# Two padding tiles in a one-core trunk kernel: where the tiles that TensorE reads begin in a partition

## Chip, core and metric

The program runs on one core of one Trainium2 chip. The metric is device time in microseconds (us) of one execution, from the launch to the end; lower is better. A profiled execution has a span too: the time from the first to the last instruction that the hardware profiler recorded. Engines are named as in the profile: PE is TensorE's matmul side, PEld its weight loads, DVE is VectorE, ACT is ScalarE, POOL is GpSimd, SP is SyncE, which here issues nearly all DMAs.

## What is computed

A decoder trunk of two layers on a sequence of 256 tokens with 1024 features, all in 32-bit floats. Each layer is half a SwiGLU feed-forward block, a mixer, and another half feed-forward block; layer 0 mixes by latent attention beside a pooling mixer, layer 1 by a causal spatial gate:

```python
def _swiglu(x, w_gate, w_up, w_down):
    return (jax.nn.silu(x @ w_gate) * (x @ w_up)) @ w_down

for layer in range(DEPTH):                       # DEPTH = 2
    h = h + 0.5 * _swiglu(_rmsnorm(h, ffn_norm[layer, 0]), ...)   # 1024 -> 2816 -> 1024
    hn = _rmsnorm(h, mix_norm[layer])
    h = h + (_mla_pool_mixer(hn, ...) if layer % 2 == 0 else _spatial_gating_mixer(hn, ...))
    h = h + 0.5 * _swiglu(_rmsnorm(h, ffn_norm[layer, 1]), ...)
```

## The kernel before

Everything is held transposed: features lie on the 128 partitions and the 256 tokens along them. The kernel keeps 32-bit accuracy by splitting each operand in two values of type float32r, a rounded high part and a low part that is the rest. A weight chunk arrives from HBM in a tile `raw` of 128 x 1024 floats (`emit_dma`, L148, issued by SP), ACT casts it to `whi` (`emit_hi`, L160, L169), and DVE subtracts to get `wlo` (`emit_split`, L171, L177). There are five buffers of `raw` and six each of `whi` and `wlo`; `next_chunk` (L196) keeps this pipeline some chunks ahead of the use. The activations are split likewise: a tile `x` holds for each of eight feature blocks the low part and then the high part, 256 tokens each. `pp` is the same for the hidden layer of a feed-forward block, `comb` and `zz` for the mixers (they use the buffers of `x`).

Two helpers make nearly all products. `mm2` (L214) serves the feed-forward blocks. It issues two matmuls for each weight block of 128 columns: one with `wlo` as the stationary operand and the 256 columns of the high activations moving (L216), and one with `whi` stationary and all 512 columns, low and high, moving (L217). `mm3` (L209) serves the mixers, with three matmuls of equal width (L210, L211, L212). In most of them weights are stationary and 256 activation columns move; in the three input products with the names `lat`, `kv`/`q` and `v` the activations are stationary and 416, 512, 384 or 512 weight columns move. Each matmul has a weight load of its own. A feed-forward block runs 352 pairs of `mm2` for gate and up (`gate_up`, L341) and 176 for down (`down`, L388); there are four such blocks, so 2112 pairs in all.

The order of instructions is the order of the code (a manual schedule). Tiles come out of pools, and a pool hands out bytes of a partition in the order in which the tiles are first asked for: `const`, then `weights` (`raw`, `whi`, `wlo`), then `acts` (`x`), then `small`, and behind them the pools that live for one block (`pp`, `gu` and `a` in a feed-forward block, the mixers' tiles otherwise). A tile that is added to `const` shifts all that stands behind it.

Of the kernel before, what the change touches and what calls it, by code (L numbers as in the profile page):

```python
# [9 lines left out]
F32 = mybir.dt.float32  # L10
# [6 lines left out]
P = 128  # L17
# [59 lines left out]
def trunk_kernel(  # L77
# [24 lines left out]
    const = ctx.enter_context(tc.tile_pool(name="const", bufs=1))  # L102
    wpool = ctx.enter_context(tc.tile_pool(name="weights", bufs=1))
    xpool = ctx.enter_context(tc.tile_pool(name="acts", bufs=1))
    spool = ctx.enter_context(tc.tile_pool(name="small", bufs=2))
# [916 lines left out]
        return nxt  # L1022


    wu = const.tile([P, T], mybir.dt.bfloat16, name="wu")
    nc.vector.memset(wu, 0.0)
    warm_ps = acc_bank()
# [118 lines left out]
```

## Time and profile before

| | us |
|---|---|
| device time, median of 3 runs (lowest, highest) | 909.73 (909.56, 912.51) |
| device time of the profiled execution | 912.56 |
| its span | 910.8 |
| outside the span | 1.8 |
| PE busy | 899.7 |
| DVE busy | 645.5 |
| ACT busy | 496.4 |

Matmuls overlap in the pipeline, so "busy" counts an engine with at least one matmul in flight. How fast PE goes is read from the starts: the distance between the start of one matmul and the start of the next is what one costs in a stream. The timeline has these starts to 0.01 us, so a distance is best taken over many rows. The recorded duration of a single matmul (281 ns or 399 ns, say) is longer than this distance, since it holds the way through the pipeline.

### The profile page before, as it was taken

How to read it: one execution, taken by the hardware profiler on the slowest of the kernel's cores; microseconds unless marked ns; L12 is line 12 of the kernel's file. 1: busy time of each engine (PE TensorE's matmuls, PEld its weight loads, DVE VectorE, ACT ScalarE, POOL GpSimd, SP SyncE). 2: the span in 40 equal slices, each digit the busy share in tenths (PEclk: the TensorE clock that was granted, in tenths of full speed). 3: DMA queues.
4: the chain of work that ended last, by engine and by line, in shares of the span. 5: the costliest groups of instructions: out<-in, count | busy, mean ns of one | idle time of the engine just before them, and what ended most of it. 6: DMA issues, size and time to landing. Idle time of an engine off the chain costs nothing.

```text
span 910.8 us, 13887 instructions
## 1 busy us (share of the span) xinstructions
PE 899.7 (99%) x5320; PEld 790.6 (87%) x5320; DVE 645.5 (71%) x973; ACT 496.4 (55%) x782; POOL 99.5 (11%) x130
## 2 busy tenths in 40 slices
PE   8999999999999999999999999999999999999998
PEld 6888888899898888888888888888899988888887
DVE  7787778668877877785558777756658768777652
ACT  8555554447675555554446555544445655555430
POOL 4200000017524000000030000000120220000000
PEclk9999999999999999999999999999999999999999
DMA  8575555634344655556544555576446446555740
GB/s 290 189 241 192 195 178 192 210 120 159 116 140 139 203 182 190 178 188 234 192 157 141 185 185 185 185 258 185 157 148 202 144 160 206 188 186 186 248 162 23
DMA packets 59281, 164.45 MB, mean 181 GB/s; under 512 B 5456, under 2 KB 7760, under 8 KB 59216
## 3 DMA queue, kind: packets, MB, share of 16 engines
q1 hardware_dynamic: 59216, 163.58, 53.3%
q8 instruction: 41, 0.67, 0.3%
q14 instruction: 24, 0.20, 0.1%
HBM read 162.51 MB, written 1.05 MB: 180 GB/s over the span
## 4 chain that ended last, share of the span: by engine, by line
PE 95%; DVE 1%; POOL 1%; issue 1%; DMA 0%; ACT 0%; SPq 0%; DVEq 0%
PE rot L217 27%; PE acc L217 26%; PE rot L216 14%; PE acc L216 13%; PE acc L211 3%; PE acc L210 3%; PE acc L212 2%; PE rot L210 2%; PE rot L212 2%; PE rot L211 2%; DMA raw<-w_gu 0%; PE rot L973 0%; POOL diag L297 0%; DVE wlo L182 0%; PE rot L821 0%
## 5 line engine op out<-in xcount | busy, mean ns | idle before, releaser
L177 DVE TENSOR_TENSOR wlo<-raw,whi 128x1024 fp32r<-128x1024 f32 (+2 forms) x298 | 352.9, 1228 | 78.0 <-ACT whi L169 77.9
L169 ACT CAST whi<-raw 128x1024 fp32r<-128x1024 f32 (+2 forms) x303 | 301.0, 1043 | 109.0 <-PE acc L217 40.6
L217 PE MATMUL rot<-x,whi 128*128 128x512 f32 x704 | 249.8, 399 | 0.0
L217 PE MATMUL acc<-x,whi 128*128 128x512 f32 x704 | 249.7, 398 | 0.0
L216 PE MATMUL acc<-x,wlo 128*128 128x256 f32 x704 | 198.3, 282 | 2.4 <-DVE wlo L182 2.4
L216 PE MATMUL rot<-x,wlo 128*128 128x256 f32 x704 | 197.9, 281 | 0.0
L217 PEld LDWEIGHTS rot<-x,whi 128*128 128x128 f32 x704 | 132.3, 188 | 32.6
L217 PEld LDWEIGHTS acc<-x,whi 128*128 128x128 f32 x704 | 132.3, 188 | 32.2
L216 PEld LDWEIGHTS acc<-x,wlo 128*128 128x128 f32 x704 | 133.0, 189 | 3.6 <-DVE wlo L182 3.5
L216 PEld LDWEIGHTS rot<-x,wlo 128*128 128x128 f32 x704 | 133.0, 189 | 0.0
L217 PE MATMUL rot<-pp,whi 128*128 128x512 f32 x352 | 124.5, 397 | 0.0
L217 PE MATMUL acc<-pp,whi 128*128 128x512 f32 x352 | 124.5, 397 | 0.0
L216 PE MATMUL rot<-pp,wlo 128*128 128x256 f32 x352 | 99.1, 281 | 0.0
L216 PE MATMUL acc<-pp,wlo 128*128 128x256 f32 x352 | 99.1, 281 | 0.0
L217 PEld LDWEIGHTS acc<-pp,whi 128*128 128x128 f32 x352 | 66.1, 188 | 16.4
L217 PEld LDWEIGHTS rot<-pp,whi 128*128 128x128 f32 x352 | 66.1, 188 | 16.4
L216 PEld LDWEIGHTS acc<-pp,wlo 128*128 128x128 f32 x352 | 66.4, 189 | 0.0
L216 PEld LDWEIGHTS rot<-pp,wlo 128*128 128x128 f32 x352 | 66.4, 189 | 0.0
L359 ACT COPY a<-rot 128x256 f32<-128x256 f32 x88 | 30.0, 372 | 57.7 <-PE rot L217 57.7
L359 ACT COPY a<-acc 128x256 f32<-128x256 f32 x88 | 30.0, 372 | 55.2 <-PE acc L217 55.2
L361 DVE TENSOR_TENSOR gu<-rot,a 128x256 f32<-128x256 f32 x88 | 31.5, 419 | 36.3 <-ACT a L359 36.3
L278 POOL TENSOR_TENSOR sqsum<-sq,sq 128x256 f32<-128x256 f32 x6 | 6.1, 1011 | 459.6 <-ACT sq L273 459.6
(246 smaller groups left out, 1037.1 us busy)
## 6 DMA issues: line engine op xcount, KB each, us to landing
raw<-w_gu SPq DMA_DIRECT2D x172, 512.0 KB, 4.6
raw<-w_down SPq DMA_DIRECT2D x88, 512.0 KB, 4.6
raw<-ew_out SPq DMA_DIRECT2D x8, 512.0 KB, 3.5
raw<-ow_v SPq DMA_DIRECT2D x8, 512.0 KB, 4.3
raw<-ow_u SPq DMA_DIRECT2D x8, 512.0 KB, 6.0
raw<-ow_out SPq DMA_DIRECT2D x8, 512.0 KB, 4.2
raw<-ew_p SPq DMA_DIRECT2D x4, 512.0 KB, 4.2
raw<-w_gu SPq DMA_DIRECT2D x7, 256.0 KB, 4.6
```

The lines of the kernel that those rows point to most:

```text
L169: nc.scalar.copy(hi[:, :n], r[:, :n])
L177: eng.tensor_sub(lo[:, :n], r[:, :n], hi[:, :n].bitcast(F32))
L210: nc.tensor.matmul(out, wl, xh, start=start, stop=False, skip_group_check=True)
L211: nc.tensor.matmul(out, wh, xl, start=False, stop=False, skip_group_check=True)
L212: nc.tensor.matmul(out, wh, xh, start=False, stop=stop, skip_group_check=True)
L216: nc.tensor.matmul(bank[:, 0:T], wl, x[:, 1, :], start=start, stop=False, skip_group_check=True)
L217: nc.tensor.matmul(bank, wh, x.rearrange("p s t -> p (s t)"), start=False, stop=stop, skip_group_check=True)
L278: nc.gpsimd.tensor_add(t, s.sum, sq)
L359: nc.scalar.copy(a[:, i, :], bank[:, 0:T])
L361: nc.vector.tensor_add(gu[:, i, :], bank[:, T:], a[:, i, :])
```

## The change

Two tiles are asked for and never used: one of 352 bytes per partition at the end of `const`, and one of 32 bytes at the end of `small`. No instruction is added, removed or moved: on each of the five engines the list of operations, with their operands' names and waits, is the same before and after.

```diff
+    const.tile([P, 88], F32, name="align")
+    spool.tile([P, 8], F32, tag="align", name="align_small", bufs=1)
     wu = const.tile([P, T], mybir.dt.bfloat16, name="wu")
     nc.vector.memset(wu, 0.0)
```

What moves are addresses. This is the remainder of the first byte of each tile, in its partition, by 512; it follows from the sizes of the tiles in the order of the pools. All buffers of one name have the same remainder, and the slices that `mm2` and `mm3` take of `x`, `pp`, `whi` and `wlo` lie whole multiples of 512 bytes behind the start, except the second half of a `lat` chunk (128 bytes more).

| tile | before | after |
|---|---|---|
| `raw`, `whi`, `wlo`, `x` (`comb`, `zz`), `wu` | 160 | 0 |
| `pp`, `ckvh`, `ckvl`, `cqh`, `cql`, `wt`, odd mixer's `v_sb` | 128 | 0 |
| `gu`, `a`, `u_sb`, `z` (not read by PE) | 128 | 0 |
| `qT`, `kT`, `lat`, even mixer's `v_sb` | 384 | 256 |
| `qnat`, `knat`, `sm`, `pT`, `on` | 448 | 320 |
| `sqsum` | 160 | 32 |
| `diag` | 416 | 288 |
| `par_h`, `cst_sb`, `ones_r`, `cmean`, `pool_w_sb` | 128, 416, 256, 256, 128 | the same |

So the operands of L210 to L212, L216 and L217 all begin on a multiple of 512 bytes after the change (the odd halves of `lat` chunks apart); those of the small transposes, scores and row sums do not.

## Rows read from the trace of the kernel before

**Rows 1.** The page's part 1 (busy us of each engine, share of the span, instructions) and, from part 2, the granted TensorE clock in 40 slices of the span, in tenths of full speed.

```profile
PE 899.7 (99%) x5320; PEld 790.6 (87%) x5320; DVE 645.5 (71%) x973; ACT 496.4 (55%) x782; POOL 99.5 (11%) x130
...
PEclk9999999999999999999999999999999999999999
```

**Rows 2.** The page's part 4, the chain of work that ended last, as shares of the span by engine and by line.

```profile
PE 95%; DVE 1%; POOL 1%; issue 1%; DMA 0%; ACT 0%; SPq 0%; DVEq 0%
PE rot L217 27%; PE acc L217 26%; PE rot L216 14%; PE acc L216 13%; PE acc L211 3%; PE acc L210 3%; PE acc L212 2%; PE rot L210 2%; PE rot L212 2%; PE rot L211 2%; DMA raw<-w_gu 0%; PE rot L973 0%; POOL diag L297 0%; DVE wlo L182 0%; PE rot L821 0%
```

**Rows 3.** The waits of PE over the whole span: who waited for whom, us in total, times, longest us.

```profile
PE acc L216 <- DVE wlo L182: 2.4, 3, 1.8
PE acc L302 <- POOL diag L297: 1.4, 1, 1.4
PE acc L1030 <- DVE wu L1026: 1.0, 1, 1.0
```

**Rows 4.** Groups of PE's instructions by line and shape over the whole span: names, shapes, count, then busy us and mean ns of one, then idle us before them. First the pairs of `mm2`, then `mm3` of the odd mixer with 256 and with 512 moving columns, then the scores of the attention, which are plain 32-bit floats (each such product has two records).

```profile
L217 PE MATMUL rot<-x,whi 128*128 128x512 f32 x704 | 249.8, 399 | 0.0
L217 PE MATMUL acc<-x,whi 128*128 128x512 f32 x704 | 249.7, 398 | 0.0
...
L217 PE MATMUL rot<-pp,whi 128*128 128x512 f32 x352 | 124.5, 397 | 0.0
L217 PE MATMUL acc<-pp,whi 128*128 128x512 f32 x352 | 124.5, 397 | 0.0
...
L212 PE MATMUL acc<-zz,whi 128*128 128x256 f32 x64 | 18.1, 283 | 0.0
...
L212 PE MATMUL rot<-whi,x 128*128 128x512 f32 x32 | 12.5, 390 | 0.0
...
L821 PE MATMUL rot<-kT,qT 96*128 96x256 f32 x16 | 4.8, 380 | 0.0
...
L820 PE MATMUL rot<-kT,qT 96*128 96x128 f32 x16 | 3.1, 273 | 0.0
```

**Rows 5.** The timeline of PE from 300 to 322 us, in a gate-and-up stretch: start us, us of one, operation. The first six rows and the last; from the first to the last it is 63 pairs of L216 and L217, alternating.

```profile
299.74 0.28 PE L216 MATMUL rot<-x,wlo 128*128 128x256 f32 x1
299.86 0.40 PE L217 MATMUL rot<-x,whi 128*128 128x512 f32 x1
300.09 0.28 PE L216 MATMUL rot<-x,wlo 128*128 128x256 f32 x1
300.20 0.40 PE L217 MATMUL rot<-x,whi 128*128 128x512 f32 x1
300.44 0.28 PE L216 MATMUL rot<-x,wlo 128*128 128x256 f32 x1
300.55 0.40 PE L217 MATMUL rot<-x,whi 128*128 128x512 f32 x1
...
322.00 0.28 PE L216 MATMUL rot<-x,wlo 128*128 128x256 f32 x1
```

**Rows 6.** The same from 150 to 172 us, in a down stretch, where `pp` moves. From the first row of L217 to the last one it is 62 pairs.

```profile
149.95 0.39 PE L217 MATMUL rot<-pp,whi 128*128 128x512 f32 x1
150.18 0.28 PE L216 MATMUL rot<-pp,wlo 128*128 128x256 f32 x1
...
171.86 0.39 PE L217 MATMUL acc<-pp,whi 128*128 128x512 f32 x1
```

**Rows 7.** The timeline of PE near the start of the program, from the first pair after a wait for data. From the second row to the last it is 9 pairs of the same tiles `x`, `whi` and `wlo`.

```profile
8.11 0.39 PE L216 MATMUL acc<-x,wlo 128*128 128x256 f32 x1 [1.77 <-DVE wlo L182]
...
8.57 0.28 PE L216 MATMUL acc<-x,wlo 128*128 128x256 f32 x1
...
11.70 0.27 PE L216 MATMUL acc<-x,wlo 128*128 128x256 f32 x1
```

**Rows 8.** The timeline of PE in the odd mixer, `mm3` with 256 moving columns of `x` and stationary `whi` or `wlo`: first and last row, 17 matmuls apart.

```profile
689.77 0.28 PE L210 MATMUL acc<-x,wlo 128*128 128x256 f32 x1
...
691.81 0.28 PE L212 MATMUL acc<-x,whi 128*128 128x256 f32 x1
```

**Rows 9.** The timeline of PE in the odd mixer's `v` product, `mm3` with 512 moving columns of `whi` or `wlo` and stationary `x`: first and last row, 40 matmuls apart.

```profile
654.82 0.39 PE L212 MATMUL rot<-whi,x 128*128 128x512 f32 x1
...
663.89 0.39 PE L210 MATMUL rot<-whi,x 128*128 128x512 f32 x1
```

**Rows 10.** The timeline of PE in the even mixer's `kv` product, with 512 moving columns of `whi` or `wlo` and stationary `ckvh` or `ckvl`: the first row of 12 and the row after the twelfth.

```profile
213.66 0.39 PE L210 MATMUL acc<-whi,ckvl 128*128 128x512 f32 x1
...
216.45 0.34 PE L210 MATMUL rot<-whi,cql 128*128 128x384 f32 x1
```

**Rows 11.** The timeline of PE at one head's scores: two records of 128 columns of plain 32-bit floats, then two of 256.

```profile
234.75 0.39 PE L820 MATMUL rot<-kT,qT 96*128 96x128 f32 x2
234.97 0.60 PE L821 MATMUL rot<-kT,qT 96*128 96x256 f32 x2
```

**Rows 12.** The chain that ended last in order of time (start us, us, what): one of its pieces at the start of the program. It is the longest DMA on it.

```profile
3.53 4.52 DMA raw<-w_gu
```

**Rows 13.** The two costliest groups of the page's part 5: line, engine, operation, shapes, count, busy us and mean ns of one, then idle us and what ended the idle time.

```profile
L177 DVE TENSOR_TENSOR wlo<-raw,whi 128x1024 fp32r<-128x1024 f32 (+2 forms) x298 | 352.9, 1228 | 78.0 <-ACT whi L169 77.9
L169 ACT CAST whi<-raw 128x1024 fp32r<-128x1024 f32 (+2 forms) x303 | 301.0, 1043 | 109.0 <-PE acc L217 40.6
```

## The prediction

> **What bounds the kernel now.** I read the page first. PE has work in flight for 99% of the span, and the granted clock is at the full level, 2.4 GHz, in every slice [rows 1]. The chain that ended last is PE's for 95%, and L216 and L217 alone hold 80% of the span [rows 2]. PE's longest wait class comes to 2.4 us, at the start of the program [rows 3]. So the time is the number of matmuls times their distance in the stream, and other engines matter only where they would stop PE.
>
> The distances come from the timeline. A pair of `mm2` in a gate-and-up stretch costs 22.26 us / 63 = 353.3 ns [rows 5]. In a down stretch it costs 21.91 us / 62 = 353.4 ns [rows 6]. The 2112 pairs [rows 4] at 353.3 ns make 746 us of the 910.8 us. At 2.4 GHz and one column per cycle a pair's 256 + 512 columns would take 320 ns, so each pair holds 33 ns that are not columns. `mm3` has the same kind of excess: 2.04 us / 17 = 120.0 ns for 256 columns, where 106.7 ns are columns [rows 8], and 9.07 us / 40 = 226.8 ns for 512 columns, where 213.3 ns are columns [rows 9]. In both it is 13 ns, once per matmul and not per column. The whole question of this change is whether these 13 to 17 ns per matmul hang on where the operands begin.
>
> **What the change does to each part.** It adds and removes no instruction, so there is no new wait and nothing passes anything in a queue. It can act only through addresses. I go through the readers and writers of the shifted tiles.
>
> Matmul streams, first the moving operand. Before the change the trace holds both a moving tile that begins at remainder 160 (`x`) and one at 128 (`pp`), against the same stationary tiles at 160. The first is a multiple of 32 bytes only, the second of 128. If PE read in units of 64 or 128 bytes and paid for a start inside a unit, the pairs with `pp` would be cheaper. They cost 353.4 ns against 353.3 ns [rows 5, 6]: no difference in a tenth of a nanosecond over 60 pairs. So no unit up to 128 bytes shows for the moving operand.
>
> Then the stationary operand. `ckvh` begins at 128 and is stationary where 512 columns of `whi` move: 2.79 us / 12 = 232.5 ns [rows 10]. `x` at 160 is stationary in the same shape in the `v` product at 226.8 ns [rows 9]. The better aligned one is slower by 6 ns, so this gives no gain either. Neither comparison reaches units of 256 or 512 bytes: no large operand begins on one now. For those I have only an indirect bound, the sign that the excess varies at fixed addresses. Just after the program's start the same `x`, `whi` and `wlo` make pairs of 3.13 us / 9 = 347.8 ns [rows 7], 5.5 ns less than the steady 353.3 ns. At least that part is set by something other than the start address.
>
> Bounds of the matmul term, both ways. Most that can be gained: plain 32-bit scores, whose operands begin at 384, a multiple of 128, cost 0.22 us / 2 = 110 ns for a record of 128 columns [rows 11], and 380 - 273 = 107 ns more for 128 columns more [rows 4], so 3 ns are left over per record. They take two cycles for each column, so their reads come half as fast, and they are no fair model of a float32r stream. If a float32r matmul too came down to 3 ns above its columns, a pair would fall by 33.3 - 6 = 27.3 ns, 57.7 us over 2112 pairs. The 672 `mm3` matmuls of 256 columns (counted in the code) would fall by 10.3 ns, 6.9 us, and the 108 of 512 columns by about 11 ns, 1.2 us. That is 66 us in all. Most that can be lost: the 5.7 ns between the two stationary tiles, on every L217, 2112 x 5.7 = 12 us. My value is zero, because the one direct comparison at equal shape and equal neighbours (`x` against `pp`) is the nearest row, and it shows zero.
>
> The Trainium skill, "TensorE: Matmul & The Clock Gate", section "Back-to-back issue gap", speaks against that value. It puts a warm isolated matmul at its columns over 2.4 GHz plus about 2.5 ns, with no term for a weight load or an address, so a pair would be 325 ns, an estimate from that page. The trace disagrees with the page by 28 ns per pair, and the page doesn't say why. If address alignment were the whole reason, the sum by the page would be 60 us less for the pairs.
>
> DMA. `raw` moves from 160 to 0, so each row of 4096 bytes lands on other boundaries. Transfers are hidden behind PE except at the start, where one lies on the chain for 4.52 us [rows 12]. No row shows one landing at another remainder. I bound it by a twentieth of this piece either way, 0.2 us, since the bytes and the packets stay as they are; I take 0.
>
> The Trainium skill, "DMA: Bandwidth & Descriptors", section "How a descriptor splits into AXI transactions", says that a start off a 256-byte boundary costs an extra partial transaction. For 4096 bytes from remainder 160 that is 133 beats in place of 128, an estimate from the page, 4% of a transfer. No row here can show it.
>
> ACT and DVE read and write the shifted tiles too, 1043 ns and 1228 ns for a chunk of 1024 columns [rows 13]. A chunk of gate-and-up feeds 8 pairs, 2.83 us of PE, so a tenth more on either would stay hidden, and a tenth less would end no wait of PE. I take 0. The same cover holds if PE gets faster: at 325 ns per pair a chunk still lasts 2.6 us against 1.23 us on DVE plus its share of the epilogues, so a gain on PE would mostly arrive at the end.
>
> The sum: 912.56 us of the profiled execution (910.78 us of span, 1.78 us outside), 0 for the matmuls, 0 for the rest. The median of the three runs is 909.73 us, 2.8 us below the profiled one, and the forecast carries the zero over to it: **909.7 us**. Its own range is 907 to 913 us, the spread of the runs shown and the small terms.
>
> **Rivals.**
>
> *The excess is alignment, all of it.* The unit would be 256 or 512 bytes, which both 160 and 128 miss alike. For it: the excess is a fixed amount per matmul, as an extra access at a tile's edge would be; the plain 32-bit records with operands at 384 have only 3 ns; `pp` and `x` cannot tell, since both are off such a unit. Against it: the 347.8 ns at the start, and that 384 is off 256 and 512 as well, so the cheap records are no example of a good start. It gives 909.7 - 66 = 844 us. The rule of the page above would give about the same.
>
> *Part of it is alignment.* One of the two streams, or only what makes the steady 353.3 ns out of the 347.8 ns. The second alone is 5.5 ns x 2112 = 11.6 us, 898 us; half of the 66 us would be 877 us. For it: the distances are not constant, L216's 0.12 us and then 0.11 us, L217's 0.23 us and then 0.24 us within three pairs [rows 5], so the two reads keep some rhythm that could be changed.
>
> *Slower, because all streams now begin at the same place of a unit.* The two reads of PE, moving and stationary, would meet at their starts. Place: every L217, where a weight load runs beside 512 moving columns. Price: the 5.7 ns by which the `kv` product is dearer than the `v` product [rows 9, 10], its stationary tile being the one with the rounder address, so 12 us and 922 us. For it: this is the only row in which an operand nearer to a round address costs anything. Against it: `x` and `whi` already share the remainder 160 and pay no more than `pp` and `whi`, which do not. It decides from 1.3 ns per pair on, which is 2.7 us.
>
> *The change does not do what it says.* The small tiles of attention and row sums stay off 512. The scores are a rounded 0% of the chain [rows 2], so this alters nothing here.
>
> **How the numbers follow.** About 0.3% (2.7 us) is what a measurement of this kernel can tell from no change. No change by my direct rows: 0.53. All of the excess: 0.12. A part of it, 877 to 903 us: 0.20. Slower by 3 to 15 us: 0.15, most of it up to 922 us, a little of it above. The range runs from 876 to 923 us: it takes in the forecast, the partial gains and most of the slower case, and leaves out the full gain and the rest, under 0.2. Faster by over 0.3%: 0.32. Within: 0.53. Slower: 0.15.
>
> **What would show it.** In the profile of the changed kernel the distance of L216/L217 pairs decides: 353 ns in both stretches if I am right, 326 ns for the full rival, 342 to 348 ns for a part, 357 ns or more for the slower one. If only the moving operand counts, pairs and both shapes of `mm3` all fall; if only weight loads count, the 256-column matmuls, which leave a weight load the least cover, should fall and the 512-column ones hardly. If PE's distance falls and the time does not, waits of PE for `whi` or `wlo` must appear. What would make me wrong is a unit of 256 bytes or more, of which no large operand of this trace stands on the good side.

## The result and the profile after

The changed kernel took 904.57 us as the median of six runs (902.79 to 906.24), the kernel before 912.56 us beside it (909.56 to 913.28). The ratio is 0.992, with a 95% interval of 0.9896 to 0.9945: faster by 0.8%, some 7 to 8 us. The forecast of no change did not come. The time lies in the stated range, 876 to 923 us, but below the 907 to 913 us that the forecast of no change gave itself. The runs do not scatter evenly. Those of the changed kernel are 902.79, 902.85, 903.11 and 906.03, 906.19, 906.24; those of before are 909.56, 909.73 and 912.51 to 913.28. They stand on steps about 3.2 us apart.

The profiled execution took 906.19 us, 6.37 us less than the profiled one of before. The page's part 1 and the longest waits of PE (us, times, longest us), to be held against [rows 1, 3]:

```profile
PE 894.2 (99%) x5320; PEld 787.5 (87%) x5320; DVE 645.7 (71%) x973; ACT 496.1 (55%) x782; POOL 99.7 (11%) x130
```

```profile
PE acc L216 <- DVE wlo L182: 1.4, 4, 0.4
PE acc L302 <- POOL diag L297: 1.4, 1, 1.4
PE acc L1033 <- DVE wu L1029: 1.0, 1, 1.0
```

PE still has work in flight for 99% of the span and has no more to wait for than it had. So the gain must be in the distance of its matmuls. The timeline of the second feed-forward block of the changed kernel, gate and up, the stretch of [rows 5] (start us, us, operation):

```profile
299.76 0.28 PE L216 MATMUL rot<-x,wlo 128*128 128x256 f32 x1
299.88 0.39 PE L217 MATMUL rot<-x,whi 128*128 128x512 f32 x1
300.11 0.27 PE L216 MATMUL rot<-x,wlo 128*128 128x256 f32 x1
...
321.95 0.28 PE L216 MATMUL rot<-x,wlo 128*128 128x256 f32 x1
```

From the first row to the last it is 64 pairs: 22.19 / 64 = 346.7 ns, where [rows 5] gave 353.3 ns. The same for the third block:

```profile
499.77 0.28 PE L216 MATMUL rot<-x,wlo 128*128 128x256 f32 x1
499.89 0.40 PE L217 MATMUL rot<-x,whi 128*128 128x512 f32 x1
...
521.68 0.28 PE L216 MATMUL rot<-x,wlo 128*128 128x256 f32 x1
```

Here it is 62 pairs, 21.91 / 62 = 353.4 ns, the old distance, with operands that begin on a multiple of 512 bytes as well. Over the whole trace the first and the third block run at 353.3 ns and the second and the fourth at 346.7 ns, each in gate-and-up and down alike. In a block this holds from the 48th pair on, behind the row that spreads the norm (L302, L303). Two blocks x 480 pairs x 6.67 ns = 6.4 us: the whole difference of the two profiled executions.

The third block shows where the distance changes. Its timeline around L302 and L303:

```profile
473.42 0.28 PE L216 MATMUL rot<-x,wlo 128*128 128x256 f32 x1
473.53 0.39 PE L217 MATMUL rot<-x,whi 128*128 128x512 f32 x1
473.76 0.28 PE L216 MATMUL rot<-x,wlo 128*128 128x256 f32 x1
...
474.46 0.28 PE L302 MATMUL acc<-diag,ones_r 128*128 128x256 f32 x1
474.57 0.28 PE L303 MATMUL acc<-diag,ones_r 128*128 128x256 f32 x1
...
475.39 0.28 PE L216 MATMUL rot<-x,wlo 128*128 128x256 f32 x1
475.51 0.40 PE L217 MATMUL rot<-x,whi 128*128 128x512 f32 x1
475.75 0.28 PE L216 MATMUL rot<-x,wlo 128*128 128x256 f32 x1
475.87 0.40 PE L217 MATMUL rot<-x,whi 128*128 128x512 f32 x1
476.10 0.28 PE L216 MATMUL rot<-x,wlo 128*128 128x256 f32 x1
476.22 0.40 PE L217 MATMUL rot<-x,whi 128*128 128x512 f32 x1
476.45 0.28 PE L216 MATMUL rot<-x,wlo 128*128 128x256 f32 x1
```

The pair ahead of L302 that is shown takes 0.34 us, and the 14 pairs between the row sums and L302 take 347.1 ns each on average. Behind L303 the pairs take 0.36, 0.35 and 0.35 us, over and over: 1.06 us for three, where three at the shorter distance take 1.04. Nothing waits there and the tiles are the same. The stream comes out of the two foreign matmuls in another rhythm than it went in with, and the block keeps it.

Two theories stood against each other. **A:** the start address sets the distance of a pair, and a multiple of 512 bytes is the good one. **B:** a stream of pairs has two rhythms, 346.7 and 353.3 ns, that keep themselves up; which one a block runs in is drawn anew at each interruption, and moved addresses only change the draw.

### The profile page after: what moved, and what is told of

Its sections match the earlier page's. It is cut to its first block, busy times and chain, and to the rows that moved or that the text cites. A ratio compares the mean times of both kernels' runs of the same rounds, so it can differ in the third digit from the quotient of the medians.

```text
span 904.4 us, 13887 instructions
## 1 busy us (share of the span) xinstructions
PE 894.2 (99%) x5320; PEld 787.5 (87%) x5320; DVE 645.7 (71%) x973; ACT 496.1 (55%) x782; POOL 99.7 (11%) x130
## 4 chain that ended last, share of the span: by engine, by line
PE 94%; DVE 2%; POOL 1%; issue 1%; ACT 1%; DMA 1%; SPq 0%; DVEq 0%; POOLq 0%
PE rot L217 27%; PE acc L217 26%; PE rot L216 13%; PE acc L216 13%; PE acc L211 3%; PE acc L210 3%; PE acc L212 2%; PE rot L210 1%; PE rot L211 1%; PE rot L212 1%; DMA raw<-w_gu 1%; PE rot L973 0%; POOL diag L297 0%; DVE wlo L182 0%; PE rot L821 0%
## 5 line engine op out<-in xcount | busy, mean ns | idle before, releaser
L217 PE MATMUL acc<-x,whi 128*128 128x512 f32 x704 | 248.3, 397 | 0.0
L217 PE MATMUL rot<-x,whi 128*128 128x512 f32 x704 | 247.6, 396 | 0.0
L216 PE MATMUL acc<-x,wlo 128*128 128x256 f32 x704 | 197.7, 281 | 1.4 <-DVE wlo L182 1.4
L216 PE MATMUL rot<-x,wlo 128*128 128x256 f32 x704 | 196.6, 279 | 0.0
L217 PEld LDWEIGHTS acc<-x,whi 128*128 128x128 f32 x704 | 132.6, 188 | 31.3
L217 PEld LDWEIGHTS rot<-x,whi 128*128 128x128 f32 x704 | 132.2, 188 | 31.6
L216 PEld LDWEIGHTS acc<-x,wlo 128*128 128x128 f32 x704 | 133.1, 189 | 2.9 <-DVE wlo L182 2.9
L216 PEld LDWEIGHTS rot<-x,wlo 128*128 128x128 f32 x704 | 132.6, 188 | 0.0
L217 PE MATMUL rot<-pp,whi 128*128 128x512 f32 x352 | 123.4, 396 | 0.0
L217 PE MATMUL acc<-pp,whi 128*128 128x512 f32 x352 | 123.4, 396 | 0.0
L216 PE MATMUL acc<-pp,wlo 128*128 128x256 f32 x352 | 98.2, 279 | 0.0
L216 PE MATMUL rot<-pp,wlo 128*128 128x256 f32 x352 | 98.2, 279 | 0.0
L217 PEld LDWEIGHTS rot<-pp,whi 128*128 128x128 f32 x352 | 66.1, 188 | 15.9
L217 PEld LDWEIGHTS acc<-pp,whi 128*128 128x128 f32 x352 | 66.1, 188 | 15.9
L216 PEld LDWEIGHTS rot<-pp,wlo 128*128 128x128 f32 x352 | 66.3, 188 | 0.0
L216 PEld LDWEIGHTS acc<-pp,wlo 128*128 128x128 f32 x352 | 66.3, 188 | 0.0
```

Of the source, the lines that this page charges most:

```text
L216: nc.tensor.matmul(bank[:, 0:T], wl, x[:, 1, :], start=start, stop=False, skip_group_check=True)
L217: nc.tensor.matmul(bank, wh, x.rearrange("p s t -> p (s t)"), start=False, stop=stop, skip_group_check=True)
```

## The experiments

Eleven kernels were run, and three of them were profiled a second time. This table gathers what their profiles show: the remainders by 512 at which the large operands begin (`whi`, `wlo`, `x`, then `pp`, with which `ckvh` and `ckvl` of the even mixer go), the span of the profiled execution, the rhythm of the four feed-forward blocks behind L303, and all times. "5" stands for 346.7 ns to the block's end, "-" for 353.3 ns, "u" for 346.7 ns in gate-and-up and 353.3 ns in down (in "row later" the third block takes up its rhythm at its 89th pair). The rhythms are mean distances of the starts of L216 in the trace; each lies within 0.2 ns of one of the two values.

| kernel | remainders | span, us | blocks | all runs, us |
|---|---|---|---|---|
| before | 160, 128 | 910.8 | - - - - | 909.6 to 913.3 beside the change; 906.0 to 913.3 in all (64) |
| the change | 0, 0 | 904.4 | - 5 - 5 | 902.8 to 903.1 (3), 906.0 to 906.2 (3) |
| all at 256 | 256, 256 | 907.8 | - - 5 - | 909.4 to 909.7 (6) |
| all at 64 | 64, 64 | 900.8 | - 5 5 5 | 899.8, 902.6, 903.5, 906.0, 906.5, 909.5 |
| first tile alone | 0, 480 | 911.0 | - - - - | 907.5 to 912.8 (12) |
| second tile alone | 160, 160 | 901.4 | 5 5 5 - | 902.9 to 903.2 (4) |
| row later | 160, 128 | 907.4 | - - 5 - | 906.0 to 912.4 (12) |
| row as a pair | 160, 128 | 904.7 | 5 5 - - | 904.1 to 910.4 (12) |
| second tile, row as a pair | 160, 160 | 899.3 | 5 5 5 5 | 900.1 to 901.1 (5) |
| row's first half twice | 160, 128 | 903.5 | - 5 5 u | 902.8 to 910.8 (12) |
| change, row as a pair | 0, 0 | 904.7 | - 5 - 5 | 903.4 to 903.7 (4), 906.5 (2) |
| all at 64, again | 64, 64 | 904.6 | 5 - 5 - | 906.4 |
| before, again | 160, 128 | 909.3 | - u - - | 911.1 |
| the change, again | 0, 0 | 911.0 | - - - - | 912.7 |

With a span of 910.9 us for no block, 3.2 us off for each "5" (480 pairs) and 2.0 us off for a "u" (304 pairs x 6.67 ns), and 0.6 us or 0.7 us on for the added columns, every span is met within 0.6 us.

**All large operands at 256.** The sizes of the padding are changed:

```diff
-    const.tile([P, 88], F32, name="align")
+    const.tile([P, 24], F32, name="align")
```

> All large operands begin at remainder 256: const padded by 96 bytes, small by 32. Theory A (the start address sets the distance of the pairs, and a multiple of 512 is the good one): 353.3 ns per pair in all four feed-forward blocks, time as before, about 912.6 us. Theory A with a unit of 256 bytes: as the change, 346.7 ns in the second and fourth block, 902.8 to 906.2 us. Theory B (a stream of pairs runs in one of two rhythms, 353.3 or 346.7 ns, that a whole block keeps; an address shift only changes which one a block falls into): any number n of blocks at 346.7 ns, each worth about 490 pairs x 6.7 ns = 3.3 us, so 912.6 - 3.3 n us, and runs of the same kernel that differ by multiples of 3.3 us.

It took 909.53 us, ratio 0.997 (0.9959 to 0.9981), with the third block alone at 346.7 ns. A start on 256 is no rule for either distance: three blocks have one, and one block the other.

**All large operands at 64.** As before, with 104 in place of 24.

> All large operands begin at remainder 64: const padded by 416 bytes, small by 32. Theory A: as before, about 912.6 us, 353.3 ns in all blocks, unless 64 bytes are the unit, then 902.8 to 906.2 us as the change. Theory B: 912.6 - 3.3 n us with some n from 0 to 4, each block wholly at 353.3 or 346.7 ns behind its interruption by the norm.

It took 904.75 us, ratio 0.9917 (0.989 to 0.9944), and its six runs stand on four steps from 899.8 to 909.5 us. One program, one set of addresses, and 9.7 us, three blocks' worth, between its fastest and its slowest run: theory A has no place for that.

**The first padding tile alone.**

```diff
-    spool.tile([P, 8], F32, tag="align", name="align_small", bufs=1)
```

> The first padding tile alone: whi, wlo, x at 0, pp at 480. Theory A: gate and up pairs (both operands at 0) as in the change, down pairs (pp at 480) at 353.3 ns, so a gain two thirds of the change's, 905 to 907.5 us, and blocks whose distance changes between gate-and-up and down. Theory B: a block keeps its rhythm through both parts though pp lies elsewhere; 912.6 - 3.3 n us.

It took 911.87 us, ratio 0.9993 (0.9978 to 1.0008). All blocks of the profile run at 353.3 ns, gate-and-up with both operands at 0 among them. So the tile that brings `whi`, `wlo` and `x` to a multiple of 512 gains nothing by itself.

**The second padding tile alone.**

```diff
-    const.tile([P, 88], F32, name="align")
```

> The second padding tile alone: whi, wlo, x stay at 160, pp moves from 128 to 160, and nothing is on a multiple of 64. Theory A: no gain, 912.6 us, 353.3 ns in all blocks. Theory B: 912.6 - 3.3 n us; a block at 346.7 ns here would show that no rounder start is needed for it.

It took 903.11 us, ratio 0.99 (0.9887 to 0.9912), no less gain than the change had, with every large operand at 160. Its timeline in the second and in the fourth block:

```profile
299.75 0.39 PE L217 MATMUL rot<-x,whi 128*128 128x512 f32 x1
299.98 0.28 PE L216 MATMUL rot<-x,wlo 128*128 128x256 f32 x1
...
321.94 0.39 PE L217 MATMUL rot<-x,whi 128*128 128x512 f32 x1
...
799.72 0.28 PE L216 MATMUL acc<-x,wlo 128*128 128x256 f32 x1
799.84 0.40 PE L217 MATMUL acc<-x,whi 128*128 128x512 f32 x1
...
821.98 0.28 PE L216 MATMUL acc<-x,wlo 128*128 128x256 f32 x1
```

22.19 us / 64 pairs is 346.7 ns, and 22.26 us / 63 pairs is 353.3 ns. In gate-and-up `x`, `whi` and `wlo` lie here at the very addresses of the kernel before. This falls out of theory A altogether. What the second tile does do is to bring `pp`, and `ckvh` and `ckvl` of the even mixer, to the remainder of `x` and `whi`. (It is asked for ahead of the other tiles of `small`, not at the end of that pool, so `sqsum` and `diag` move by 32 bytes too.) So there is a rival that theory A does not name: not a round start, but equal remainders. It comes back below.

**The row of the norm eight pairs later**, addresses as before. `mid` holds the row and, behind it, the first epilogue of the block, so that moves too:

```diff
-{0: lambda: norm_sum(s, bank), 2: mid} if b == 1 else {}
+{0: lambda: norm_sum(s, bank), 3: mid} if b == 1 else {}
```

> Addresses as in the kernel before; the row that spreads the norm (L302, L303) is issued a quarter of a block later. Theory A (start addresses set the distance): 353.3 ns in all four blocks, 912.6 us. Theory B (two rhythms, drawn at the interruption by L302 and L303): the draw is made at another moment, so some n of the blocks may run at 346.7 ns, 912.6 - 3.3 n us; n = 0 would not speak against it, n > 0 would speak against A.

It took 909.17 us beside 909.66 us for the kernel before, ratio 0.9985 (0.9967 to 1.0004): the median tells nothing. The profile does. In the third block the rhythm changed not at L302 but 12 us later, at pair 89, where a weight load had to wait 0.29 us for `wlo`. The rows of L217 on both sides of it in the timeline of PE, and the row of the weight load:

```profile
480.83 0.40 PE L217 MATMUL rot<-x,whi 128*128 128x512 f32 x1
...
490.73 0.40 PE L217 MATMUL acc<-x,whi 128*128 128x512 f32 x1
...
491.66 0.40 PE L217 MATMUL acc<-x,whi 128*128 128x512 f32 x1
...
513.85 0.39 PE L217 MATMUL acc<-x,whi 128*128 128x512 f32 x1
```

```profile
491.09 0.19 PEld L216 LDWEIGHTS acc<-x,wlo 128*128 128x128 f32 x1 [0.29 <-DVE wlo L177]
```

Ahead of the wait it is 28 pairs in 9.90 us, 353.6 ns; behind it 64 pairs in 22.19 us, 346.7 ns, and so to the end of the block. The first block went the other way at the same pair, after a wait of 0.49 us for the same tile; a wait of 0.29 us in the second block changed nothing. In the fourteen profiles the distance changes where the stream is broken: behind a mixer, at the row sums (L284), at L302 and L303, and at a wait, as here or in the first microseconds. It also changes in four places where nothing breaks the stream and only the moving tile becomes another one, `pp` for `x` or `x` for `pp`; one is shown below. As long as the tiles stay the same and nothing comes between, it never changes.

**The row shaped as one more pair**, addresses as before. The high half is spread first, then one 512-column matmul adds the low half and writes columns that nobody reads:

```diff
-        nc.tensor.matmul(bc, ones_r, s.dg[:, 1], start=True, stop=False, ...)
-        nc.tensor.matmul(bc, ones_r, s.dg[:, 0], start=False, stop=True, ...)
+        nc.tensor.matmul(bc, ones_r, s.dg[:, 0], start=True, stop=False, ...)
+        nc.tensor.matmul(s.bank, ones_r, s.dg.rearrange("p s t -> p (s t)"), start=False, stop=True, ...)
```

> Addresses as in the kernel before; L302 stays a 256-column matmul and L303 becomes a 512-column one, so that the interruption has the shape of one more pair. It adds 6 x 107 ns = 0.6 us of columns. Theory A: 353.3 ns in all blocks, 913.2 us. Theory B: the rhythm ahead of L302 goes on behind it; the second and the fourth block run at 346.7 ns just ahead of L302 in the trace of the kernel before and then stay there, the third takes over the second's rhythm: n = 2 or 3, 903 to 907 us.

It took 907.0 us, ratio 0.9973 (0.9953 to 0.9994), with two blocks at 346.7 ns at the old addresses. But one part of my theory B fell: the rhythm ahead of L302 was not carried over it. The second block went from 353.3 to 346.7 ns, the third and the fourth the other way. Even behind a break in the shape of a pair the rhythm can be another.

**The second tile and the pair-shaped row together.**

> The second padding tile alone (large operands at 160, 903.1 us) and the pair-shaped row. Theory A': its addresses are what is good, so 903.1 + 0.6 = 903.7 us, the fourth block at 353.3 ns. Theory B: the fourth block keeps the 346.7 ns that it had ahead of L302, all four blocks at 346.7 ns, 903.7 - 3.3 = 900.4 us.

It took 900.32 us, ratio 0.9888 (0.9869 to 0.9908), all five runs within 1.1 us and all four blocks at 346.7 ns. The time was met, the reason given for it not: ahead of L302 the fourth block ran at 353.3 ns. It is the fastest median of the study (the changed kernel did not run beside it), and none of its large operands begins on a multiple of 64. A row of its fourth block and the one 64 pairs later, 22.19 us apart:

```profile
799.80 0.28 PE L216 MATMUL acc<-x,wlo 128*128 128x256 f32 x1
...
821.99 0.28 PE L216 MATMUL acc<-x,wlo 128*128 128x256 f32 x1
```

**The first half of the row issued twice**, addresses as before:

```diff
+        nc.tensor.matmul(bc, ones_r, s.dg[:, 1], start=True, stop=False, ...)
         nc.tensor.matmul(bc, ones_r, s.dg[:, 1], start=True, stop=False, ...)
```

> Addresses as in the kernel before; L302 is issued twice (the first is overwritten), 6 x 0.12 us = 0.7 us more. Theory A: 353.3 ns in all blocks, 913.3 us. Theory B: another draw at each interruption, 913.3 - 3.3 n us with n from 0 to 4.

It took 905.91 us, ratio 0.9943 (0.9925 to 0.9962): six more matmuls and no other edit made the kernel 0.6% faster, at addresses that the change calls bad.

Its fourth block shows a change of rhythm that no break explains. These are rows of PE around the end of gate-and-up:

```profile
815.32 0.28 PE L216 MATMUL acc<-x,wlo 128*128 128x256 f32 x1
...
837.16 0.27 PE L216 MATMUL rot<-x,wlo 128*128 128x256 f32 x1
837.27 0.40 PE L217 MATMUL rot<-x,whi 128*128 128x512 f32 x1
837.50 0.28 PE L216 MATMUL acc<-pp,wlo 128*128 128x256 f32 x1
837.62 0.39 PE L217 MATMUL acc<-pp,whi 128*128 128x512 f32 x1
...
859.76 0.28 PE L216 MATMUL acc<-pp,wlo 128*128 128x256 f32 x1
```

The 64 pairs up to 837.50 us take 22.18 us, 346.6 ns each; the 63 pairs behind it take 22.26 us, 353.3 ns each. No other matmul comes between, and neither PE nor its weight loads wait. What is new is the moving tile: `x` begins at remainder 160, like `whi` and `wlo`, and `pp` at 128.

**The change with the pair-shaped row.**

> The change's addresses (large operands at 0) and the row of the norm shaped as one more pair (L303 with 512 columns, 0.6 us more columns). Theory A (a multiple of 512 is good): no better than the same shape at remainder 160, which took 900.3 us with all four blocks at 346.7 ns, if that is where the gain ends; worse than it would count against A again. Theory B (two rhythms, drawn at each interruption): some n from 0 to 4, 906.8 us for n = 2, 903.5 for n = 3, 900.2 for n = 4. If equal remainders of all large operands plus the pair shape are what makes the draw good, n = 4.

It took 903.68 us, ratio 0.9921 (0.9899 to 0.9942), two blocks at 346.7 ns in the profile. Equal remainders and this shape are not enough for all four blocks; with 160 in place of 0 they had all four.

**Three kernels again**, unchanged, one execution each.

> The same program as with all operands at 64, run once more. Its six runs lay from 899.8 to 909.5 us. Theory A: the same distances in the same blocks as in its first profile (first block 353.3 ns, the others 346.7). Theory B: the blocks may differ from the first profile although no address differs.

906.40 us, the first and the third block at 346.7 ns, where the first profile of the same program had the second, third and fourth.

> The kernel before, run once more. Its runs beside the last experiments lay at 906.0 to 907.2, 909.2 to 910.1 and 912.4 to 913.2 us. Theory A: 353.3 ns in all four blocks. Theory B: if the profiled run lies at 909.3 us, one block is at 346.7 ns with all operands at their old addresses; at 912.7 us none is, which tells nothing.

911.12 us: the kernel before itself has a stretch at 346.7 ns. Its second block, first in gate-and-up, then in down:

```profile
299.78 0.28 PE L216 MATMUL rot<-x,wlo 128*128 128x256 f32 x1
...
321.97 0.28 PE L216 MATMUL rot<-x,wlo 128*128 128x256 f32 x1
...
419.81 0.28 PE L216 MATMUL acc<-pp,wlo 128*128 128x256 f32 x1
...
441.72 0.28 PE L216 MATMUL rot<-pp,wlo 128*128 128x256 f32 x1
```

64 pairs in 22.19 us (346.7 ns), then 62 pairs in 21.91 us (353.4 ns).

> The changed kernel, run once more. Its six runs lay at 902.8 to 903.1 or 906.0 to 906.2 us. Theory A: first and third block at 353.3 ns, second and fourth at 346.7, as in its first profile. Theory B: at 906 us two blocks at 346.7 ns, at 903 us three, not always the same ones.

912.74 us, all four blocks at 353.3 ns, as slow as the kernel before. The second block of the changed kernel, to be held against the stretch at 346.7 ns of its first profile above:

```profile
299.66 0.40 PE L217 MATMUL rot<-x,whi 128*128 128x512 f32 x1
...
321.92 0.40 PE L217 MATMUL rot<-x,whi 128*128 128x512 f32 x1
```

22.26 us / 63 pairs = 353.3 ns. The addresses of the change do not secure its gain.

## Why the prediction was right and wrong

*What bounds the kernel.* Right. PE's stream is the time, and what changed is the distance of its matmuls alone: 960 pairs x 6.67 ns is 6.4 us, the profiled difference.

*No unit of the start address shows, for either operand.* Right for the pairs, and now for larger units too. The two distances are the same two, 346.7 and 353.3 ns, at remainders 0, 64, 160 and 256. A multiple of 512 left the pair at 353.3 ns in two blocks of the change, in all four of its second profile, and in all four with the first tile alone. `mm3` with 512 columns of `v` stands where it stood: 41 matmuls in 9.30 us are 226.8 ns [rows 9].

```profile
650.68 0.39 PE L211 MATMUL rot<-wlo,x 128*128 128x512 f32 x1
...
659.98 0.39 PE L210 MATMUL rot<-whi,x 128*128 128x512 f32 x1
```

*The value zero.* This is the step that failed. I took 353.3 ns as what a pair of these tiles costs, since [rows 5, 6] agreed; behind L303 all four blocks of that trace do run at it. But it is no constant: the second profile of the same kernel has a stretch at 346.7 ns, and the trace that I had read has one too, just ahead of L302 in its second block:

```profile
285.11 0.28 PE L216 MATMUL acc<-x,wlo 128*128 128x256 f32 x1
...
289.97 0.28 PE L216 MATMUL acc<-x,wlo 128*128 128x256 f32 x1
```

That is 14 pairs in 4.86 us, 347 ns each. A row that hinted at it was on the table: 347.8 ns at the start of the program, at the same addresses [rows 7]. I used it rightly to say that 5.5 ns are set by something else than the address, and then booked these 5.5 ns as a rival in which alignment removes them. The right question was what else can move a pair between the two values, and whether any edit could do so by accident. The size of that rival was near, 11.6 us for all 2112 pairs at 5.5 ns, where the runs give 6.67 ns x 480 pairs = 3.2 us per block, 12.8 us for four. But it is luck that the time lay in the range: the lower end had been set for gains by a rounder start, and nothing in the runs shows that a rounder start brought any.

*The rival that all the excess is alignment.* It fell: no pair came below 346.7 ns as a steady distance. The Trainium skill, "TensorE: Matmul & The Clock Gate", section "Back-to-back issue gap", has a formula by which a pair would take 325 ns, an estimate from that page. The section gives it for a single isolated matmul and says that a stream of weight loads and matmuls is paced by both, so it was no measure for this stream, and the prediction overlooked that. The trace stays 22 ns above it even in the shorter rhythm, at every remainder that was run.

*The slower rival.* It fell, and the reading under it was wrong. It took the `kv` product for 5.7 ns dearer than the `v` product because its stationary tile is the rounder one, and it feared equal remainders. But in `v` both operands begin at 160, and in `kv` before the change they differ, `whi` at 160 and `ckvh` at 128. With both on 0 the `kv` product costs 2.77 us / 12 = 230.8 ns [rows 10]:

```profile
213.83 0.39 PE L210 MATMUL acc<-whi,ckvl 128*128 128x512 f32 x1
...
216.60 0.33 PE L210 MATMUL rot<-whi,cql 128*128 128x384 f32 x1
```

The fourteen profiles separate cleanly: in the six in which the two operands begin at different remainders the twelve matmuls take 2.79 or 2.80 us, in the eight with equal ones 2.74 to 2.77 us. The kernel with the row as a pair and the one with the second tile added to it differ by that tile alone. Their rows, first without it, then with it:

```profile
210.44 0.39 PE L210 MATMUL acc<-whi,ckvl 128*128 128x512 f32 x1
...
213.23 0.34 PE L210 MATMUL rot<-whi,cql 128*128 128x384 f32 x1
```

```profile
211.46 0.39 PE L210 MATMUL acc<-whi,ckvl 128*128 128x512 f32 x1
...
212.84 0.39 PE L210 MATMUL acc<-whi,ckvl 128*128 128x512 f32 x1
...
214.20 0.33 PE L210 MATMUL rot<-whi,cql 128*128 128x384 f32 x1
```

That is 2.79 us against 2.74 us, and with the tile the last six matmuls take 1.36 us, 226.7 ns each, the distance of the `v` product. So a start address does show here, not by its roundness but by whether the moving and the stationary tile share a remainder by 512. In this product it is worth some 0.05 us.

*DMA, ACT and DVE at zero.* Right: the pairs alone make the whole difference, the median chunk of `w_gu` lands after 4.6 us in both profiles, DVE is busy for 645.7 us against 645.5 us, ACT for 496.1 us against 496.4 us.

*What is shown and what is open.* Shown: the two rhythms; that both appear at fixed addresses from run to run; that edits which leave every address alone change which of them a block runs in; that a multiple of 512 does not decide between them. Not settled: what in TensorE keeps a rhythm up, and what decides which one a break leaves behind. It is no even toss: in all fourteen profiles the second and the fourth block open at 353.3 ns behind the mixer and hold it for 32 pairs.

The odds differ between programs. The kernel with the second tile and the pair-shaped row had about the same time in all its five runs, and the change fell well in six of seven, where the kernel before took 908.3 us or more in 60 of its 64 runs, so that at most little more than one block's worth was won in them. Equal remainders may have a part in this. In the eight profiles in which `pp` shares the remainder of `x` and `whi`, all 17 blocks that had 346.7 ns in gate-and-up kept it through down; in the six in which it doesn't, 5 of 7 did. The second block runs on into the third without a break, from `pp` back to `x`: with equal remainders the shorter rhythm was kept in 5 of 5, with different ones in none of 2. But equal remainders alone do not bring the shorter rhythm: the kernel with all at 256 has it in one block only, and the second profile of the change in none. Nor are they needed: the two kernels with an edited row and the old addresses have it in two blocks and in three, one of these in gate-and-up alone. How much of the 7 to 8 us is due to them stays open; a kernel with `pp` alone moved, run often enough to count blocks, would tell.

## What to carry to other kernels

Take the distance of matmul starts block by block before pricing a layout: if the same tiles show two distances in one trace, the difference is not the price of the tiles but a state of the stream, and an edit that has nothing to do with it can win or lose it. Where runs of one program stand on even steps, look in the profile for the stretch that is worth one step, and do not credit an edit with a step until a second profile of the same program agrees. An edit that only moves addresses needs a control that moves them elsewhere; here the control at 160 bytes won no less than the alignment did. And ask not only how round a start is, but whether the tiles that are read together begin at the same remainder: the first question found nothing here, the second one did.

## What the runs showed of the hardware

I had not expected that a dense stream of float32r matmuls, at the full granted clock and with nothing to wait for, has two steady paces 1.9% apart (346.7 and 353.3 ns for 768 columns), that it holds either through a block of 166 us, and that a break of two matmuls or a 0.29 us wait is enough to go over from one to the other. Nor had I expected that twelve matmuls of 512 columns take 2.79 or 2.80 us where the moving and the stationary tile begin at different remainders by 512 bytes (160 and 128, or 0 and 480), and 2.74 to 2.77 us where they share one (0, 64, 160 or 256).
